# A PEER decoder layer on one core: map jobs begin earlier, weight splits a half unit later, a transfer on another queue, the last norm's splits placed by hand

## The chip, the cores and the metric

The kernel runs on one core of a Trainium2 chip. The metric is the time of one execution on the device in microseconds (us); less is better. Three runs of the kernel before took 2154.39 to 2157.17 us, median 2155.43 us. The profile comes from one more execution.

## What is computed

One decoder layer for T = 320 tokens (256 of a prompt, 64 of samples), D = 2048: a mixer (attention and a gated unit), then PEER, then a gated per-layer embedding (PLE). What matters here is PEER: each token picks 8 x 16 of 16384 experts, each expert being one row of `u_tab` and one of `v_tab`. The last two lines are the stage behind it.

```python
def one_block(xb):
    q = jnp.einsum('td,de->te', xb, wq).reshape(PEER_BLOCK, PEER_HEADS, 2, PEER_HALF)
    s1 = jnp.einsum('thc,nc->thn', q[:, :, 0], k1).astype(jnp.float32)
    s2 = jnp.einsum('thc,nc->thn', q[:, :, 1], k2).astype(jnp.float32)
    v1, i1 = lax.top_k(s1, PEER_TOPK)
    v2, i2 = lax.top_k(s2, PEER_TOPK)
    ...
    e = (jnp.take_along_axis(i1, ci // PEER_TOPK, axis=-1) * N_KEYS
         + jnp.take_along_axis(i2, ci % PEER_TOPK, axis=-1))
    g = jax.nn.softmax(sc, axis=-1).astype(xb.dtype)
    ue = jnp.take(u_tab, e, axis=0)
    act = jax.nn.gelu(jnp.einsum('thkd,td->thk', ue, xb))
    ve = jnp.take(v_tab, e, axis=0)
    return jnp.einsum('thk,thkd->td', g * act, ve)
...
h = h + peer(rmsnorm(h, norm_ffn), peer_wq, peer_k1, peer_k2, peer_u, peer_v)
gate = jax.nn.sigmoid(jnp.einsum('bld,de->ble', rmsnorm(h, ple_gate_norm), ple_gate_w))
h = h + jnp.einsum('blp,pd->bld', ple, ple_w) * gate
```

## The kernel before

**Units.** For 240 of the tokens the experts are computed densely. The tables are cut into 256 units of 1 MB: 128 u units (2048 x 128 of `u_tab`, then a gelu) and 128 v units. `order` lists them: 32 u units, then 16 groups of 8 v units with u units between. A unit has two halves, and a half two quarters. Float32 is made of two parts, so `prepare(n, h)` (L671) splits a half unit: a copy on ScalarE (ACT) gives `w_hi` (L683), a subtraction on VectorE (DVE) `w_lo` (L684). In its first half it also starts the unit's transfer `w_raw` on SyncE's queue. The pool of split halves has four buffers, so the split runs four half units ahead of `multiply(n, h, q)`, which issues a quarter: 12 matmuls on TensorE (PE), three for each of 4 chunks (`mm3`, L98 to L100). `finish(n)` (L702) evicts the unit's sum.

**The routing map.** Beside the first u units runs `front()`, the norm and the choice of the experts, a generator that tells its own cost in us at each `yield`; a loop gives it 1.4 us of such cost for each half unit. Then 30 jobs of 8 tokens build the map, the weight of each token for each expert. A job is `one_hots(j)`, two VectorE operations `e` (L762) and `p` (L763) in tiles with two buffers, and `map_products(j)`: 16 small matmuls (L775) in two groups, each with an eviction on ScalarE (L779). Every second job ends with a transfer `gd<-g_st` of 1 MB on GpSimd's (POOL) queue (L786). The one-hots of job j+1 are issued ahead of the products of job j. The jobs stand in ten half units (`first` to `U1` = 28), one or two behind each quarter, three in a half unit; `prepare(n + 2, h)` stands behind them.

**The routing weights.** Behind the map `fetch_g(0)` (L837) reads the first group's part of it back as `g_t` (960 KB, L839, on ScalarE's queue). `weights(g, gt)` (L842) is a generator of ten steps that multiplies the gelus with `g_t` (L854, VectorE) and splits the product in two (L865 ScalarE, L849 VectorE: `wh` and `wl`, or `a` and `c` for the first four). The v units multiply with these. `rows_of` (L791) makes rows of the other 80 tokens: copies `xd` on ScalarE (L801), transposes on TensorE (L798). For these tokens 160 steps (L819 a gather of rows on GpSimd's queue, L828 or L832 on VectorE) are spread over the units up to `END`, in proportion to the work planned.

**The last stage.** The pool of the PLE stage takes space that the last group's weights (`th`, `tl`) used. It loads `p_t` on GpSimd's queue (L1038), splits it in `p_h` (L118) and `p_l` (L121), multiplies with the embedding's weights (sums `ps_s`, evicted at L1046), splits the 16 chunks of the hidden state and sums their squares (L142, L143), and ends with 16 units of `w_gate`.

DVE, ACT and PE execute in the order of the code inside `manual_schedule`; the PLE stage stands behind it, and there a scheduler orders the work.

Of the kernel before, what the change touches and what calls it, by code (L numbers as in the profile page):

```python
# [10 lines left out]
F32 = mybir.dt.float32  # L11
# [41 lines left out]
def _build(ctx, tc, nc, a):  # L53
# [783 lines left out]
    def fetch_g(g):  # L837
        gt = vp.tile([P, NTB, GRP, 16], F32, name="g_t")
        nc.scalar.dma_start(gt.rearrange("p a b c -> p (a b c)"), gd[g])  # L839
        return gt  # L840

    def weights(g, gt):  # L842
# [4 lines left out]
        for i in range(GRP + 2):  # L847
# [9 lines left out]
            if 1 <= i <= GRP:  # L857
# [3 lines left out]
                elif k < 4:  # L861
                    w[k] = [flat4(up.tile([P, TD], F32R, tag="act", name=n, bufs=LEAD)) for n in ("th", "tl")]
# [5 lines left out]
    def add_samples():  # L868
        for c4 in range(2):
# [8 lines left out]
            )  # L878

# [11 lines left out]
    def front():  # L891
# [5 lines left out]
        yield 2.0  # L897
        shut(c_rt)
        state["xc"], xcp = open_pool("xc")
# [3 lines left out]
        yield 2.8  # L903
        one_hots(0)
        yield 2.8

    with tc.manual_schedule(engines={mybir.EngineType.DVE, mybir.EngineType.Activation, mybir.EngineType.PE}):
# [4 lines left out]
        steps = front()  # L912
        n, spent, slots = 0, 0.0, 0
        while steps:
            for h in range(2):
                multiply(n, h, 0)
                multiply(n, h, 1)
                if h == 0 and n:
                    finish(n - 1)
                slots += 1  # L920
                while steps and spent < 1.4 * slots:
                    cost = next(steps, None)
                    if cost is None:
                        steps = None
                    else:
                        spent += cost
                prepare(n + 2, h)
            n += 1

        first, job = n, 0  # L930
        while n < U1:
            for h in range(2):
                for q in range(2):
                    multiply(n, h, q)
                    if h == 0 and q == 0:
                        finish(n - 1)
                    at_ = (4 * (n - first) + 2 * h + q + 1) / (4 * (U1 - first))
                    while job < JOBS and job < round(JOBS * at_):
                        if job + 1 < JOBS:
                            one_hots(job + 1)  # L940
                        map_products(job)
                        job += 1
                prepare(n + 2, h)
            n += 1
# [20 lines left out]
        state["g"] = fetch_g(0)  # L965
# [3 lines left out]
        for n in range(n, LEAD):  # L969
            finish(n - 1)  # L970
            for h in range(2):
# [3 lines left out]
                if 2 * (n - U1) + h >= 5:  # L975
# [10 lines left out]
        END = len(order) - 7  # L986
# [5 lines left out]
        sums_x = None  # L992
        for n in range(LEAD, len(order)):
# [9 lines left out]
            for h in range(2):  # L1003
# [11 lines left out]
                if sums_x:  # L1015
                    next(sums_x, None)
                slots += 1
# [10 lines left out]
        finish(n)  # L1028
    shut(c_vp)
# [156 lines left out]
```

## Time and profile before

| | before |
|---|---|
| median of 3 runs | 2155.43 us (2154.39 to 2157.17) |
| profiled execution | 2153.34 us |
| its span | 2151.5 us |
| TensorE busy | 2103.3 us, 98% |
| VectorE busy | 1718.2 us, 80% |
| ScalarE busy | 1004.5 us, 47% |
| GpSimd busy | 323.8 us, 15% |

The span is the profiled execution without what lies around its first and last instruction. The granted clock is given as a share of TensorE's full speed (2.4 GHz); half of it is 1.2 GHz. A matmul's duration in the timeline overlaps the next one's; the distance of two starts is what it costs. In brackets stands how long the engine was idle before the instruction, and what ended the wait.

### The profile page before, as it was taken

Reading aid. Unit: us, or ns where it says so; the run is one execution under the profiler, and the core shown is the slowest. Engines: PE = TensorE matmul, PEld = TensorE weight load, DVE = VectorE, ACT = ScalarE, POOL = GpSimd, SP = SyncE. Lnnn points to the kernel's source line nnn. Section 1 sums busy time; section 2 is a strip of 40 time slices with the busy share of each in tenths; the row PEclk is TensorE's granted clock in tenths of the full one; section 3 lists DMA queues with packets and bytes.
Section 4 is the critical chain, followed back from the end, with each engine's and each line's share of the span. In section 5 each row is a group of like instructions: output and inputs, shape, how many; then the busy total and the mean of one; then the engine's idle time right before and its main releaser. Section 6 shows DMA issues by size and latency. Waiting matters only on the chain. (4 is left out here: it accounts for less than half of the span.)

```text
span 2151.5 us, 41052 instructions
## 1 busy us (share of the span) xinstructions
PE 2103.3 (98%) x17106; PEld 2053.0 (95%) x17106; DVE 1718.2 (80%) x2570; ACT 1004.5 (47%) x1465; POOL 323.8 (15%) x230
## 2 busy tenths in 40 slices
PE   8999999999998889999999999999999999999999
PEld 7878999999997879999999999999999999999998
DVE  6674875799997658888888888898898888886754
ACT  5346554335456655444444444444444444444632
POOL 2000000000001111221222222222222222120000
PEclk9999999999999889999999999999999999999999
DMA  7412354433555678998998989998898898895452
GB/s 279 144 59 99 115 182 172 140 121 137 188 203 168 201 255 311 365 345 333 387 353 340 376 349 336 360 374 350 336 377 338 349 383 355 312 367 181 161 181 83
DMA packets 85209, 563.06 MB, mean 262 GB/s; under 512 B 9894, under 2 KB 14438, under 8 KB 22160
## 3 DMA queue, kind: packets, MB, share of 16 engines
q1 hardware_dynamic: 49936, 349.76, 43.8%
q0 software_dynamic: 29536, 190.83, 23.4%
q10 hardware_dynamic: 5552, 19.86, 2.4%
q8 instruction: 134, 2.20, 0.4%
q14 instruction: 51, 0.42, 0.1%
HBM read 541.58 MB, written 19.79 MB: 261 GB/s over the span
## 5 line engine op out<-in xcount | busy, mean ns | idle before, releaser
L683 ACT ACTIVATE w_hi<-w_raw 128x1024 fp32r<-128x1024 f32 x512 | 542.8, 1061 | 698.9 <-PE ps_o L99 373.8
L684 DVE TENSOR_TENSOR w_lo<-w_raw,w_hi 128x1024 fp32r<-128x1024 f32 x512 | 625.3, 1222 | 218.9 <-ACT w_hi L683 216.1
L98 PE MATMUL ps_mm<-a,w_hi 128*128 128x240 f32 (+1 forms) x1776 | 519.6, 293 | 1.5 <-ACT w_hi L191 1.2
L99 PE MATMUL ps_mm<-a,w_hi 128*128 128x240 f32 (+1 forms) x1776 | 520.0, 293 | 1.0 <-DVE a L123 1.0
L100 PE MATMUL ps_mm<-a,w_lo 128*128 128x240 f32 (+1 forms) x1776 | 517.6, 291 | 2.6 <-DVE w_lo L684 2.1
L98 PE MATMUL ps_mm<-c,w_hi 128*128 128x240 f32 (+1 forms) x1280 | 361.6, 283 | 0.0
L100 PE MATMUL ps_mm<-c,w_lo 128*128 128x240 f32 (+1 forms) x1280 | 360.2, 281 | 0.0
L99 PE MATMUL ps_mm<-c,w_hi 128*128 128x240 f32 (+1 forms) x1280 | 359.9, 281 | 0.0
L99 PEld LDWEIGHTS ps_mm<-a,w_hi 128*128 128x128 f32 x1776 | 338.3, 190 | 8.9 <-issue 6.6
L98 PEld LDWEIGHTS ps_mm<-a,w_hi 128*128 128x128 f32 x1776 | 338.2, 190 | 7.8 <-issue 4.8
L100 PEld LDWEIGHTS ps_mm<-a,w_lo 128*128 128x128 f32 x1776 | 338.0, 190 | 7.0 <-issue 3.2
L81 ACT ACTIVATE w_hi<-w_raw 128x1024 fp32r<-128x1024 f32 x150 | 158.8, 1060 | 282.1 <-PE ps_mm L99 189.9
L99 PE MATMUL ps_o<-wl,w_hi 128*128 128x240 f32 x1024 | 282.9, 276 | 3.3 <-DVE wl L849 3.2
L100 PE MATMUL ps_o<-wh,w_lo 128*128 128x240 f32 x1024 | 283.0, 276 | 0.0
L98 PE MATMUL ps_o<-wh,w_hi 128*128 128x240 f32 x1024 | 279.7, 273 | 0.0
L82 DVE TENSOR_TENSOR w_lo<-w_raw,w_hi 128x1024 fp32r<-128x1024 f32 x150 | 183.0, 1223 | 89.5 <-ACT w_hi L81 86.3
L98 PEld LDWEIGHTS ps_mm<-c,w_hi 128*128 128x128 f32 x1280 | 242.8, 190 | 0.0
L100 PEld LDWEIGHTS ps_mm<-c,w_lo 128*128 128x128 f32 x1280 | 242.4, 189 | 0.2
L99 PEld LDWEIGHTS ps_mm<-c,w_hi 128*128 128x128 f32 x1280 | 242.5, 189 | 0.0
L99 PEld LDWEIGHTS ps_o<-wl,w_hi 128*128 128x128 f32 x1024 | 193.4, 189 | 4.2 <-DVE wl L849 4.0
L98 PEld LDWEIGHTS ps_o<-wh,w_hi 128*128 128x128 f32 x1024 | 194.8, 190 | 0.2 <-ACT wh L865 0.2
L100 PEld LDWEIGHTS ps_o<-wh,w_lo 128*128 128x128 f32 x1024 | 195.0, 190 | 0.0
(374 smaller groups left out, 3809.3 us busy)
## 6 DMA issues: line engine op xcount, KB each, us to landing
w_raw<-in_uT SPq DMA_DIRECT2D x128, 1024.0 KB
w_raw<-in_v_t SPq DMA_DIRECT2D x128, 1024.0 KB
w_raw<-in_w_in SPq DMA_DIRECT2D x25, 1024.0 KB
w_raw<-in_w_out SPq DMA_DIRECT2D x16, 1024.0 KB
w_raw<-in_wq SPq DMA_DIRECT2D x16, 1024.0 KB
w_raw<-in_w_gate SPq DMA_DIRECT2D x16, 1024.0 KB
gd<-g_st POOLq DMA_DIRECT2D x15, 1024.0 KB, 6.1
g_t<-gd ACTq DMA_DIRECT2D x16, 960.0 KB
```

The source lines that it names most:

```text
L81: last = act.activation(hi, s, AF.Copy)
L82: (lo_eng or vec).tensor_sub(lo, s, hi.bitcast(F32))
L98: pe.matmul(out, wh, xh, start=start, stop=False)
L99: pe.matmul(out, wh, xl, start=False, stop=False)
L100: pe.matmul(out, wl, xh, start=False, stop=stop)
L683: act.activation(hi, s, AF.Copy)
L684: vec.tensor_sub(lo, s, hi.bitcast(F32))
```

## The change

- The two loops for `front` and for the map become one over the 28 units. `front` tells less cost (1.4 for 2.0 and for 2.8; the last yield is gone), so that the jobs begin in half unit 42 instead of 46 and spread over 14 half units: two in each, but three in half units 45 and 52. In the map's half units `prepare` runs three half units ahead instead of four; half unit 41 prepares nothing, and one more `prepare` stands behind the loop.
- `fetch_g(0)` goes to GpSimd's queue. The other 15 stay on ScalarE's.
- `load`, the first group's `weights`, starts one half unit sooner.
- The last group's `th` and `tl` lie in one tile `thl` in the buffer of `xc`, which is done by then.
- `END` is ten units before the end of the order, not seven.
- `last_split()` puts the last norm's splits and squares by hand into the last seven v units, with squares of two chunks in one instruction; the loop in the PLE stage goes.

```diff
@@ -834,9 +834,9 @@
                 act.activation(self.w, self.a, AF.Gelu_apprx_tanh, scale=self.r)
                 vec.tensor_mul(self.w, self.w, self.g)
 
-    def fetch_g(g):
+    def fetch_g(g, queue=nc.scalar):
         gt = vp.tile([P, NTB, GRP, 16], F32, name="g_t")
-        nc.scalar.dma_start(gt.rearrange("p a b c -> p (a b c)"), gd[g])
+        queue.dma_start(gt.rearrange("p a b c -> p (a b c)"), gd[g])
         return gt
 
     def weights(g, gt):
@@ -859,7 +859,9 @@
                 if k < 4 and g < NG - 1:
                     w[k] = tails[k]
                 elif k < 4:
-                    w[k] = [flat4(up.tile([P, TD], F32R, tag="act", name=n, bufs=LEAD)) for n in ("th", "tl")]
+                    if k == 0:
+                        state["t"] = state["xcp"].tile([P, 8, TD], F32R, tag="xc", name="thl")
+                    w[k] = [flat4(state["t"][:, j]) for j in (2 * k, 2 * k + 1)]
                 else:
                     w[k] = [flat4(vp.tile([P, TD], F32R, name=n, bufs=GRP // 2)) for n in ("wh", "wl")]
                 act.activation(w[k][0], flat4(u[k]), AF.Copy)
@@ -877,6 +879,28 @@
                 pt.rearrange("p (c t) -> p c t", c=8),
             )
 
+    def last_split():
+
+        sq, total = {}, vp.tile([P, D], F32, tag="row", name="sqs", bufs=3)[:, : 2 * T].rearrange("p (a t) -> p a t", a=2)
+        for k in range(9):
+            if 2 <= k:
+                vec.tensor_add(total, total, sq.pop(k - 1))
+            if k < 8:
+                for c in (2 * k, 2 * k + 1):
+                    act.activation(xh(c)[0], hT[:, c], AF.Copy, scale=g_ple[:, c : c + 1])
+                yield
+                sq[k] = total
+                if k:
+                    t = vp.tile([P, D], F32, tag="row", name="sqs", bufs=3)
+                    sq[k] = t[:, : 2 * T].rearrange("p (a t) -> p a t", a=2)
+                act.activation(sq[k], hT[:, 2 * k : 2 * k + 2], AF.Square)
+                for c in (2 * k, 2 * k + 1):
+                    vec.scalar_tensor_tensor(
+                        xh(c)[1], hT[:, c], g_ple[:, c : c + 1], xh(c)[0].bitcast(F32), op0=ALU.mult, op1=ALU.subtract
+                    )
+                yield
+        vec.tensor_add(ssq, total[:, 0], total[:, 1])
+
     def add_first():
         pt = psum("tr", NC_ * XT)
         for c in range(NC_):
@@ -894,54 +918,52 @@
             yield from c
         yield from soften()
         picks = key_tables()
-        yield 2.0
+        yield 1.4
         shut(c_rt)
-        state["xc"], xcp = open_pool("xc")
+        state["xc"], state["xcp"] = open_pool("xc")
+        xcp = state["xcp"]
         state["rows"] = [xcp.tile([P, D], F32, name=n) for n in ("xc", "xx")]
         state["xd"] = lambda: xcp.tile([P, P], F32, name="xd", bufs=2)
         open_tables(picks)
-        yield 2.8
+        yield 1.4
         one_hots(0)
-        yield 2.8
 
     with tc.manual_schedule(engines={mybir.EngineType.DVE, mybir.EngineType.Activation, mybir.EngineType.PE}):
         for n in range(2):
             for h in range(2):
                 prepare(n, h)
 
-        steps = front()
-        n, spent, slots = 0, 0.0, 0
-        while steps:
+
+        steps, spent, job, first = front(), 0.0, 0, None
+        for n in range(U1):
             for h in range(2):
-                multiply(n, h, 0)
-                multiply(n, h, 1)
-                if h == 0 and n:
-                    finish(n - 1)
-                slots += 1
-                while steps and spent < 1.4 * slots:
-                    cost = next(steps, None)
-                    if cost is None:
-                        steps = None
-                    else:
-                        spent += cost
-                prepare(n + 2, h)
-            n += 1
-
-        first, job = n, 0
-        while n < U1:
-            for h in range(2):
+                slot = 2 * n + h
                 for q in range(2):
                     multiply(n, h, q)
-                    if h == 0 and q == 0:
+                    if h == 0 and q == 0 and n:
                         finish(n - 1)
-                    at_ = (4 * (n - first) + 2 * h + q + 1) / (4 * (U1 - first))
-                    while job < JOBS and job < round(JOBS * at_):
-                        if job + 1 < JOBS:
-                            one_hots(job + 1)
-                        map_products(job)
-                        job += 1
-                prepare(n + 2, h)
-            n += 1
+                    if first:
+                        at_ = (2 * (slot - first) + q + 1) / (2 * (2 * U1 - first))
+                        while job < JOBS and job < round(JOBS * at_):
+                            if job + 1 < JOBS:
+                                one_hots(job + 1)
+                            map_products(job)
+                            job += 1
+                if first:
+                    prepare((slot + 3) // 2, 1 - h)
+                else:
+                    while steps and spent < 1.4 * (slot + 1):
+                        cost = next(steps, None)
+                        if cost is None:
+                            steps = None
+                        else:
+                            spent += cost
+                    if steps:
+                        prepare(n + 2, h)
+                    else:
+                        first = slot + 1
+        prepare(U1 + 1, 1)
+        n = U1
         shut(oh["close"])
         c_vp, vp = open_pool("vp")
         c_xc, (xc, xx) = state["xc"], state["rows"]
@@ -962,7 +984,7 @@
                 rows[m] = k.fetch(j, second)
 
 
-        state["g"] = fetch_g(0)
+        state["g"] = fetch_g(0, pool)
         to_c = rows_of(xc, state["xd"], slice(TP, T), 2)
         to_x = rows_of(xx, state["xd"], slice(0, XT), PH)
         load = weights(0, state["g"])
@@ -972,7 +994,7 @@
                 for q in range(2):
                     multiply(n, h, q)
                     next(to_c, None)
-                if 2 * (n - U1) + h >= 5:
+                if 2 * (n - U1) + h >= 4:
                     for _ in range(3):
                         next(load, None)
                 if n == LEAD - 1 and h == 0:
@@ -983,13 +1005,14 @@
             pass
 
 
-        END = len(order) - 7
+        END = len(order) - 10
         extra = lambda n: 0.65 * (order[n - 1][0] == "v")
         step_us = 2.4
         total = sum(extra(n) for n in range(LEAD, END)) + 0.8 * GRP * NG + step_us * len(steps)
         m, spent, slots = 0, 0.0, 0
         sums_c = add_samples()
         sums_x = None
+        last_norm = last_split()
         for n in range(LEAD, len(order)):
             finish(n - 1)
             if order[n][0] == "v" and order[n][2] == 0:
@@ -1014,6 +1037,8 @@
                     next(sums_c, None)
                 if sums_x:
                     next(sums_x, None)
+                if order[n][0] == "v" and order[n][1] == NG - 1 and order[n][2]:
+                    next(last_norm)
                 slots += 1
                 while m < len(steps) and (spent + step_us / 2 < total * slots / (2 * (END - LEAD)) or n >= END):
                     k, j, second = steps[m]
@@ -1026,6 +1051,8 @@
                 if n + 2 < len(order):
                     prepare(n + 2, h)
         finish(n)
+        for _ in last_norm:
+            pass
     shut(c_vp)
     shut(c_xc)
     shut(c_up)
@@ -1044,9 +1071,6 @@
             for c in range(2):
                 mm3(pp, w_ple(2 * (o % 8) + c), p_hl[0][:, c], p_hl[1][:, c], c == 0, c == 1)
             act.activation(emb[:, o], pp, AF.Copy)
-        for c in range(NC_):
-            hilo(xh(c), hT[:, c], g_ple[:, c : c + 1])
-            square_sum(pl, ssq, hT[:, c], c == 0)
         pm = psum("tr", T)
         pe.matmul(pm, ones_d, ssq, start=True, stop=True)
         r = rstd(pl, pm, T)
```

VectorE's queue at the start of the map. L743 and L750 belong to `front`; `w_lo` is a split, `e` and `p` the one-hots of one job. Before:

```order
L743 CAST i_6912<-c_iota 128x512
L750 SCALAR_TENSOR_TENSOR sel_6914<-ps_tr,sel_6914 128x16x8
L750 SCALAR_TENSOR_TENSOR sel_6915<-ps_tr,sel_6915 128x16x8
L684 TENSOR_TENSOR w_lo<-w_raw,w_hi 128x1024 x2
L762 TENSOR_TENSOR e<-i_6912,sel_6914 128x2048
L763 TENSOR_TENSOR p<-e,sel_6914 128x2048
L684 TENSOR_TENSOR w_lo<-w_raw,w_hi 128x1024 x4
L762 TENSOR_TENSOR e<-i_6912,sel_6914 128x2048
L763 TENSOR_TENSOR p<-e,sel_6914 128x2048
L762 TENSOR_TENSOR e<-i_6912,sel_6914 128x2048
L763 TENSOR_TENSOR p<-e,sel_6914 128x2048
L762 TENSOR_TENSOR e<-i_6912,sel_6914 128x2048
```

And after:

```order
L743 CAST i_6912<-c_iota 128x512
L750 SCALAR_TENSOR_TENSOR sel_6914<-ps_tr,sel_6914 128x16x8
L750 SCALAR_TENSOR_TENSOR sel_6915<-ps_tr,sel_6915 128x16x8
L684 TENSOR_TENSOR w_lo<-w_raw,w_hi 128x1024
L762 TENSOR_TENSOR e<-i_6912,sel_6914 128x2048
L763 TENSOR_TENSOR p<-e,sel_6914 128x2048
L762 TENSOR_TENSOR e<-i_6912,sel_6914 128x2048
L763 TENSOR_TENSOR p<-e,sel_6914 128x2048
L762 TENSOR_TENSOR e<-i_6912,sel_6914 128x2048
L763 TENSOR_TENSOR p<-e,sel_6914 128x2048
L684 TENSOR_TENSOR w_lo<-w_raw,w_hi 128x1024
L762 TENSOR_TENSOR e<-i_6912,sel_6914 128x2048
```

One split less stands ahead of the first one-hots, which are followed at once by those of jobs 1 and 2; between two splits stand two jobs' one-hots from there on, where three jobs' stood.

ScalarE's queue at the end of the map. `g_st` are evictions of map products, `act` a gelu, `xd` a copy for a transpose. Before:

```order
L683 ACTIVATE w_hi<-w_raw 128x1024
L779 ACTIVATE g_st<-ps_o 128x4x128 x2
L779 ACTIVATE g_st<-ps_s 128x4x128 x2
L779 ACTIVATE g_st<-ps_o 128x4x128 x2
L683 ACTIVATE w_hi<-w_raw 128x1024
L839 DMA g_t<-gd 128x1920
L706 ACTIVATE act<-ps_mm 128x240
L801 ACTIVATE xd<-hT,c_gains 128x128 x2
L683 ACTIVATE w_hi<-w_raw 128x1024
L801 ACTIVATE xd<-hT,c_gains 128x128 x2
```

And after:

```order
L779 ACTIVATE g_st<-ps_s 128x4x128 x2
L779 ACTIVATE g_st<-ps_o 128x4x128 x2
L683 ACTIVATE w_hi<-w_raw 128x1024
L779 ACTIVATE g_st<-ps_s 128x4x128 x2
L779 ACTIVATE g_st<-ps_o 128x4x128 x2
L683 ACTIVATE w_hi<-w_raw 128x1024 x2
L706 ACTIVATE act<-ps_mm 128x240
L801 ACTIVATE xd<-hT,c_gains 128x128 x2
L683 ACTIVATE w_hi<-w_raw 128x1024
L801 ACTIVATE xd<-hT,c_gains 128x128 x2
```

The transfer `g_t` is gone from between the last split and the gelu, two splits stand together, and two jobs lie between splits. On GpSimd's queue it stands behind the map's transfers and ahead of the row gathers, after:

```order
L737 DMA x_eg<-ex 16x2x16 x8
L786 DMA gd<-g_st 128x16x128 x15
L839 DMA g_t<-gd 128x1920
L819 DMA row<-in_u_rows,c_e 128x2048 x64
L819 DMA row<-in_u_rows,x_eg 128x2048 x16
L819 DMA row<-in_v_rows,c_e 128x2048 x64
L819 DMA row<-in_v_rows,x_eg 128x2048 x16
L1065 DMA p_t<-in_pT 128x640
```

In before L839 is not in this queue and the gathers follow the map's transfers; the rest stands as here.

ScalarE's queue ahead of the last stage. L81 is a split of the embedding's or the gate's weights, L118 and L890 the high parts of the hidden state's chunks `c` and of `p_t`, L142 and L896 squares. Before:

```order
L81 ACTIVATE w_hi<-w_raw 128x1024 x2
L118 ACTIVATE c<-hT,c_gains 128x320 x2
L81 ACTIVATE w_hi<-w_raw 128x1024
L142 ACTIVATE sq<-hT 128x320 x6
L118 ACTIVATE p_h<-p_t 128x640
L142 ACTIVATE sq<-hT 128x320 x2
L81 ACTIVATE w_hi<-w_raw 128x1024
L142 ACTIVATE sq<-hT 128x320
L1046 ACTIVATE emb<-ps_s 128x320
```

And after:

```order
L81 ACTIVATE w_hi<-w_raw 128x1024 x2
L890 ACTIVATE c<-hT,c_gains 128x320 x2
L896 ACTIVATE sqs<-hT 128x640
L81 ACTIVATE w_hi<-w_raw 128x1024
L118 ACTIVATE p_h<-p_t 128x640
L81 ACTIVATE w_hi<-w_raw 128x1024
L890 ACTIVATE c<-hT,c_gains 128x320 x2
L896 ACTIVATE sqs<-hT 128x640
L1073 ACTIVATE emb<-ps_s 128x320 x3
```

The six squares ahead of `p_h` have become one of twice the width and the copies of two chunks, with two splits of weights behind them; evictions `emb` stand behind two more copies and a square.

## Rows read from the trace of the kernel before

**Rows 1.** the page's first line: busy time, share of the span, instructions

```profile
PE 2103.3 (98%) x17106; PEld 2053.0 (95%) x17106; DVE 1718.2 (80%) x2570; ACT 1004.5 (47%) x1465; POOL 323.8 (15%) x230
```

**Rows 2.** windows: us; busy us of PE, PEld, DVE, ACT, POOL; clock; DMA; GB/s

```profile
650.00:764.00 114.00, 95.34 (x741) 90.32 (x739) 81.64 (x69) 70.16 (x76) 17.37 (x15) 0.87 0.59 178
764.00:771.00 7.00, 0.15 (x2) 0.15 (x2) 0.33 (x1) 0.86 (x4) 1.72 (x2) 0.72 0.94 291
796.00:801.00 5.00, 2.85 (x14) 2.80 (x14) 4.40 (x5) 2.95 (x6) 0.38 (x1) 0.67 0.86 320
801.00:820.00 19.00, 19.00 (x156) 19.00 (x156) 12.91 (x14) 8.59 (x13) 4.66 (x3) 0.91 0.66 241
820.00:1960.00 1140.00, 1139.72 (x10191) 1139.53 (x10189) 992.77 (x1012) 513.55 (x647) 269.51 (x154) 1.00 0.91 351
```

**Rows 3.** timeline of PE in the map

```profile
650.75 2.05 PE L775 MATMUL ps_s<-p,e 128*128 128x128 f16 x16
666.04 2.05 PE L775 MATMUL ps_s<-p,e 128*128 128x128 f16 x16 [1.11 <-DVE p L763]
677.96 0.36 PE L98 MATMUL ps_mm<-a,w_hi 128*128 128x240 f32 x1
680.39 2.09 PE L775 MATMUL ps_s<-p,e 128*128 128x128 f16 x16
682.23 0.36 PE L98 MATMUL ps_mm<-c,w_hi 128*128 128x240 f32 x1
688.13 2.06 PE L775 MATMUL ps_s<-p,e 128*128 128x128 f16 x16 [1.08 <-DVE p L763]
759.06 2.06 PE L775 MATMUL ps_o<-p,e 128*128 128x128 f16 x16 [0.34 <-DVE p L763]
```

**Rows 4.** timeline of ACT in the map

```profile
683.36 1.06 ACT L683 ACTIVATE w_hi<-w_raw 128x1024 fp32r<-128x1024 f32 x1
```

**Rows 5.** timeline of DVE at the map's start and in it

```profile
637.19 1.22 DVE L684 TENSOR_TENSOR w_lo<-w_raw,w_hi 128x1024 fp32r<-128x1024 f32 x1 [0.17 <-ACT w_hi L683]
684.46 1.23 DVE L684 TENSOR_TENSOR w_lo<-w_raw,w_hi 128x1024 fp32r<-128x1024 f32 x1 [3.58 <-ACT w_hi L683]
```

**Rows 6.** timeline of POOL, ACT and PE at the first read of the map

```profile
762.62 1.15 POOL L786 DMA_DIRECT2D gd<-g_st  x1 [5.69 <-ACT g_st L779]
769.76 0.33 ACTq L839 DMA_DIRECT2D g_t<-gd  x1
770.14 0.37 ACT L706 ACTIVATE act<-ps_mm 128x240 f32<-128x240 f32 x1 [7.06 <-DMA gd<-g_st]
770.85 0.47 PE L798 MATMUL ps_tr<-ident,xd 128*128 128x128 f32 x1 [7.05 <-ACT xd L801]
```

**Rows 7.** the map's transfers by tile: durations ns, first and last start, landing

```profile
L786 POOL DMA_DIRECT2D gd<-g_st x15: 1152/1152/1212, 657.7 to 762.6; - x15
DMA to landing us min/median/max: 6.0/6.1/6.8
```

**Rows 8.** timeline of DVE and PE, first group's weights to their first use

```profile
786.25 0.72 DVE L854 TENSOR_TENSOR act<-act,g_t 128x240 f32<-128x240 f32 x2
797.75 0.40 DVE L849 TENSOR_TENSOR wl<-act,wh 128x240 fp32r<-128x240 f32 x1
798.20 0.57 PE L99 MATMUL ps_o<-wl,w_hi 128*128 128x240 f32 x1 [2.15 <-DVE wl L849]
```

**Rows 9.** timeline of ACT and PE before the last stage

```profile
2010.11 1.06 ACT L81 ACTIVATE w_hi<-w_raw 128x1024 fp32r<-128x1024 f32 x1 [0.31 <-ACT c L118]
2015.50 0.74 ACT L118 ACTIVATE p_h<-p_t 128x640 fp32r<-128x640 f32 x1 [0.38 <-DMA p_t<-in_pT]
2016.29 0.64 PE L98 MATMUL ps_s<-p_h,w_hi 128*128 128x320 f32 x1 [3.46 <-ACT p_h L118]
```

**Rows 10.** waits from 2004 to 2022 us: in total, times, longest

```profile
POOL p_t L1038 <- PE ps_o L100: 81.0, 1, 81.0
```

## The prediction, made before the changed kernel had run

> **What bounds the kernel now.** The page's first line comes first: TensorE is busy 98% of the span [rows 1], so only what makes it stand, or run at a lower clock, can move the time; VectorE (80%) and ScalarE (47%) count only where TensorE waits for them. The table of windows then says where it stands [rows 2]. From 820 to 1960 us it is busy 1139.72 of 1140 us at full clock: nothing is to be had there, only lost. The losses lie in four places that the change touches. While the routing map is built (650 to 764) TensorE is busy 95.34 of 114 us at a granted clock of 0.87. From 764 to 771 it does nothing. From 796 to 801 it is busy 2.85 us of 5 at clock 0.67, and 801 to 820 still shows 0.91. The fourth is a wait before the last stage [rows 9].
>
> The map first, from TensorE's timeline [rows 3]. A job (16 small matmuls) starts at 680.39 and the weight matmuls behind it at 682.23, so it holds TensorE for 1.84 us. A quarter is 12 weight matmuls; the one from 677.96 to 680.39 took 2.43 us, mostly at half clock. At full clock a matmul takes 1139.72 / 10191 = 0.112 us [rows 2], a quarter 1.34. Two quarters and two jobs are thus 6.4 us of TensorE. But the job at 688.13 starts 7.74 us after the one at 680.39, and waits 1.08 us for the one-hot product `p`. The chain between them [rows 4, 5]: job at 680.39; its evictions on ScalarE; behind them in ScalarE's queue the high half `w_hi` at 683.36 (+2.97); the low half `w_lo` on VectorE at 684.46 (+4.07); behind it the next job's `e` and `p`; the job at 688.13 (+7.74). So the split of the weights stands in the middle of the map's own chain, once in each half unit.
>
> **The map's schedule.** There are 30 jobs. Before, ten half units carry three each; after, fourteen half units, the first one four half units sooner, carry two each, but for two that carry three. The split is half a unit later, so half unit 41 splits nothing, and one `w_lo` that stood ahead of the first one-hots goes. Splitting later does not shorten the chain: in the order `w_hi` still stands behind the evictions, `w_lo` behind `w_hi`, and the one-hots behind `w_lo`. What the change does is to put each such chain beside two jobs instead of three, and to begin sooner.
> - First job. `w_lo` of 637.19 takes 1.22 us and ends at 638.4; from the end of that of 684.46 (685.7) to the job at 688.13, one-hots take 2.45 [rows 5]. So job 0 can start at 640.9 instead of 650.75 [rows 3]. Its half unit begins four half units of 2.68 us before 649.41 (650.75 less 1.34), at 638.7, and its quarter ends at 640.0: it waits 0.9 us.
> - Job 1, after one more quarter and one-hots that are ready: 640.9 + 1.84 + 1.34 = 644.1.
> - Then eleven half units of two jobs at 7.74 us = 85.1, and two of three jobs. Six jobs, two half units of before, take 666.04 to 688.13 = 22.1 us. So job 29 starts at 644.1 + 85.1 + 22.1 = 751.3 instead of 759.06: **-7.8 us**.
> TensorE has 1.3 us of slack in each half unit (7.74 - 6.4), so one quarter as slow as that of 677.96 (+1.1) is covered.
>
> **The first routing weights.** After the last job ScalarE's queue holds the issue of `g_t`, which waits for the last map transfer to land: ScalarE stands 7.06 us, and the transposes for TensorE stand behind it, so TensorE stands 7.05 us until 770.85 [rows 6]. Issued from GpSimd's queue it waits there instead; queued behind it are only the row gathers, whose rows VectorE first takes after 798. What is late next is ScalarE itself: from job 29's start its evictions (+2.97 by the chain above), two `w_hi` (1.06 each), a gelu and `xd` put the first transpose at about +5.6, against +1.84 and two quarters (+4.5) of TensorE: 1.1 to 1.3 us of the wait stay, **-5.7 us**. The clock of 0.72 there cost 3 us at half speed after 770.85; I take **-0.5 us**, since a gap stays.
>
> Does `g_t` land in time? Before, the last map transfer is issued at 762.62 (3.56 us after job 29) and has landed by 769.76 (10.7 after it). So GpSimd begins the issue at 751.3 + 10.7 = 762.0; an issue takes 1.15 us and landing 6.0 to 6.8 us for 1024 KB [rows 7]: 769.2 to 769.9. The first product with `g_t` starts at 786.25 in before [rows 8], 27.2 us after job 29; less the stall (5.7), a half unit (2.9, next part) and 0.5 that is +18.1, or 769.4. The products then have some 2 us more before TensorE needs their last result.
>
> One rule of the Trainium skill speaks against this move. The rows first: fifteen transfers of 1024 KB went out from GpSimd's queue among VectorE's one-hots, at 1152 to 1212 ns an issue and 6.0 to 6.8 us to land [rows 7], so VectorE held them up by 0.8 us at most. By "SBUF — State Buffer", section "Who interferes with whom", a transfer from GpSimd's queue can starve while VectorE works in a two-port mode, and one from ScalarE's queue can't, though the page excepts two-input operations such as the ones here. By the rule `g_t` would be late by as much as VectorE holds the port; by the row it isn't, and I go by the row.
>
> **The weights one half unit sooner.** Before, `wl` of 797.75 comes 2.15 us late for the matmul at 798.20 [rows 8], and the clock then falls: 0.67 in 796 to 801 (5 x 0.33 = 1.6, of which 0.2 lies in the wait) and 0.91 in 801 to 820 (19 x 0.09 = 1.7), 3.1 us lost [rows 2]. Starting a half unit (2.9 us) sooner, and with 12 instead of 9 turns so that nothing is left over, covers 2.15: **-2.15 and -3.1 us**.
>
> **The last norm.** Before, TensorE stands 3.46 us until 2016.29, since `p_h` at 2015.50 stands behind squares and behind the transfer of `p_t`, which waits for the last matmul of the v units [rows 9, 10]. After, `p_t` waits for ScalarE alone. A square of 640 columns (0.74 us, as `p_h`'s copy) stands ahead of the `w_hi` of 2010.11 and `p_h` right behind it: 2010.11 + 0.74 + 1.06 = 2011.9, or 2012.5 if the square waits; the first matmul comes at about 2013.0, but `p_l`, one more step on VectorE, and the evictions, behind one more chunk's copies, hold the next groups. Bounds: 0, if all that is given back, and -5, the whole wait and 1.5 us for the low clock that may follow a wait, as after 770.85; the nearest row is the wait of 3.46, less 1.5 for what is late next: **-2 us**.
>
> **The long stretch.** END three units earlier packs 160 steps 1.4% closer (3 of 217 units). VectorE is busy 992.77 of 1140 us there [rows 2]; covered by its 147 idle us, I take 0. Without the cover see the last rival. The new tiles for the last group and squares add no instruction that TensorE waits for: 0.
>
> **Sum.** -7.8 - 5.7 - 0.5 - 2.15 - 3.1 - 2 = -21.3 us. The profiled execution took 2153.34 us (span 2151.5) and would take 2132.1; the runs' median is 2155.43, 2.1 higher, so 2134.
>
> **Rivals.**
> - TensorE becomes the bound of the map: 6.4 instead of 7.74 us in a half unit, 13 x 1.3 = 17 less, some 2118. For it: jobs are sparser. Against it: the order leaves the chain whole.
> - `g_t` comes late on GpSimd's queue: the gap and low clock at `wl` stay (+5.25), 2139.5, and each us beyond another, to about 2143. For it: no margin but 2 us, and the stretch 764 to 771 has its transfers 94% busy [rows 2]. Against: 6.0 to 6.8 us in fifteen cases.
> - The waits of 1.1 to 1.3 us in each half unit bring the clock down through the whole map: two quarters at half clock (2 x 2.69) and two jobs are 9.06 us, 1.32 over 7.74: 13 x 1.32 = 17, some 2151, hardly faster. For it: before has slow quarters, as that of 677.96. Against: over the whole map of before, which has waits of 1.08 and 1.11 too, the clock is 0.87 [rows 2, 3].
> - Slower than before: the denser steps push VectorE behind, and at each of 15 groups `wl` is late as at 797.75. That wait with its clock cost 5.3 us; from 21.3 / 15 = 1.4 us a group the gain is gone, and at half the price, 2.7, the time is 2134 + 40 = 2174. Against it: TensorE idles 0.28 us in 1140 now.
>
> **Chances.** Forecast 0.62, TensorE bound 0.07, `g_t` late 0.16, low clock throughout 0.09, denser steps 0.06. A change under 0.2%, 4.3 us, can't be told from none. The forecast's own range is 2127 to 2140 (the last norm 0 to -5, the map's clock and first job +-4). For 8 in 10 I take in most of the late `g_t` and half of the faster rival: 2121 to 2145. Faster: 0.62 + 0.07 + 0.16 + half of 0.09 = 0.90; same 0.05; slower 0.05.
>
> **What would show it.** Right: jobs 7.7 us apart over a half unit, the first near 641 and the last near 751; ScalarE never waiting for the map's transfer, TensorE's gap there 1 to 1.5 us; no wait for `wl` at the first v unit; the wait for `p_h` under 1 us. Wrong: a product waiting for `g_t`, half clock in every half unit of the map, or waits for `wl` or `w_lo` between 820 and 1960.

## The result, and the profile after

The changed kernel takes 2135.67 us, the median of 4 runs (2133.95 to 2139.41), against 2155.2 us before (4 runs, 2154.39 to 2157.17): a ratio of 0.991, 95% interval 0.9893 to 0.9928. That is 19.5 us less; 2134 were forecast. Its profiled execution took 2136.97 us.

The page's first line for the changed kernel, against [rows 1]: TensorE's busy time is 2.1 us less, the span 16.3 us less. So most of what went is TensorE's standing still.

```profile
span 2135.2 us, 41032 instructions
...
PE 2101.2 (98%) x17106; PEld 2051.5 (96%) x17106; DVE 1714.6 (80%) x2563; ACT 1002.7 (47%) x1457; POOL 315.1 (15%) x231
```

The table of windows (columns as in [rows 2]), first of a stretch far ahead of the change, then of the map, what follows it, and the last stage:

```profile
184.00:194.00 10.00, 9.94 (x44) 8.11 (x44) 1.29 (x4) 4.34 (x26) 0.00 (x0) 0.66 0.00 2
643.00:755.00 112.00, 99.12 (x798) 95.08 (x798) 84.45 (x72) 71.00 (x77) 16.22 (x14) 0.94 0.62 187
755.00:761.00 6.00, 6.00 (x41) 5.99 (x39) 2.36 (x2) 5.45 (x8) 1.15 (x1) 0.72 0.83 280
761.00:781.00 20.00, 19.83 (x176) 19.45 (x174) 12.22 (x21) 14.95 (x33) 3.51 (x4) 1.00 0.99 385
781.00:786.00 5.00, 4.18 (x36) 4.03 (x37) 4.49 (x4) 3.98 (x8) 0.00 (x0) 1.00 1.01 424
806.00:1944.00 1138.00, 1137.72 (x10173) 1137.54 (x10173) 989.83 (x1012) 513.19 (x647) 260.94 (x155) 1.00 0.91 351
1996.00:2008.00 12.00, 9.21 (x42) 8.21 (x40) 9.47 (x13) 7.92 (x14) 0.00 (x0) 0.72 0.51 176
```

The same for before, of the first and the last of these stretches:

```profile
184.00:194.00 10.00, 9.88 (x63) 8.10 (x61) 2.02 (x6) 6.26 (x41) 0.00 (x0) 1.00 0.00 0
2012.00:2024.00 12.00, 8.32 (x47) 7.61 (x45) 10.01 (x19) 10.03 (x22) 0.38 (x1) 0.86 0.48 182
```

In the map TensorE is busy 99.12 of 112 us; the 7 us in which it did nothing are gone (6.00 of 6.00, at a low clock); at the first v unit 4.18 of 5 us and no low clock. The first row matters for reading all the rest: this execution ran at clock 0.66 from 184 to 194 us, where before's ran at 1.00, and lost 2.3 us before it came to anything that the change touches. So executions are compared here by stretches. Both kernels run the same 15936 weight matmuls (L98 to L100), in the same order but for some of the last stage; a stretch is the time from one of them to another, less the same in before. The borders are, in before and after: 603.56 and 605.83; the first one behind the last job, 760.87 and 755.71; the first v unit's first, 793.00 and 782.20; 809.85 and 793.29; 1944.70 and 1928.12; and the last, 2145.99 and 2130.03. The map, for one: (755.71 - 605.83) - (760.87 - 603.56) = -7.4 us. Without the 2.3 us ahead of the change the execution of after is 18.2 us shorter than that of before, for the 21.3 of the forecast.

| us against before | ahead | map | map's end to first v unit | first v unit | long stretch | last stage | sum |
|---|---|---|---|---|---|---|---|
| forecast | 0 | -7.8 | -6.2 | -5.25 | 0 | -2 | -21.3 |
| after | +2.3 | -7.4 | -5.6 | -5.8 | 0.0 | +0.6 | -16.0 |
| e1, map alone | -0.2 | -7.3 | +0.8 | -1.4 | +0.8 | +0.3 | -7.0 |
| e2, `g_t` on ScalarE | +3.3 | -7.4 | +2.3 | -5.8 | 0.0 | +0.7 | -6.9 |
| e3, weights later | +0.8 | -7.4 | -7.0 | -1.4 | +1.0 | +0.2 | -13.9 |
| e4, old last norm | -0.2 | -5.7 | -3.7 | -5.8 | 0.0 | +0.3 | -15.1 |
| e5, split early | +0.8 | -7.4 | -3.3 | -5.8 | +0.9 | +0.6 | -14.1 |
| e6, split between | +0.3 | -22.2 | -3.4 | -5.8 | 0.0 | +0.1 | -30.9 |
| e7, split ahead | -0.5 | -5.2 | -3.5 | -5.8 | +0.9 | -0.2 | -14.1 |
| e8, norm behind | +0.6 | -5.8 | -3.7 | -5.8 | +1.5 | -1.5 | -14.6 |
| e9, three edits | +0.5 | -24.2 | -6.3 | -5.8 | +1.6 | -2.4 | -36.5 |
| e10, two edits | -0.2 | -22.5 | -3.7 | -5.8 | 0.0 | -2.4 | -34.5 |
| e11, four turns | +0.5 | -7.4 | -6.1 | -5.8 | +1.3 | -0.8 | -18.3 |

In the column of the map, e4, e8 and e10 carry 1.6 us that no edit made: half clock came before their first job (0.83 from 620 to 630 us, 1.00 in after), and that job starts 38.9 us behind the first border instead of 37.3.

TensorE's timeline in the map of after, against [rows 3]: the first job, some in the middle, the last.

```profile
643.13 2.03 PE L775 MATMUL ps_s<-p,e 128*128 128x128 f16 x16 [0.67 <-DVE p L763]
646.34 2.06 PE L775 MATMUL ps_o<-p,e 128*128 128x128 f16 x16
...
654.07 2.06 PE L775 MATMUL ps_o<-p,e 128*128 128x128 f16 x16 [1.07 <-DVE p L763]
657.31 2.06 PE L775 MATMUL ps_s<-p,e 128*128 128x128 f16 x16
661.80 2.07 PE L775 MATMUL ps_o<-p,e 128*128 128x128 f16 x16 [1.08 <-DVE p L763]
...
753.90 2.06 PE L775 MATMUL ps_o<-p,e 128*128 128x128 f16 x16 [1.09 <-DVE p L763]
```

Less the 2.3 us of the start, job 0 is at 640.9, job 1 at 644.1 and the last at 751.6; forecast were 640.9, 644.1 and 751.3. From 654.07 to 661.80 it is 7.73 us, with one wait for `p` in each half unit.

### The profile page after: what moved, and what is told of

The parts are those of the page before. It is cut to its first block, busy times and chain, and to the rows that moved or that the text cites. A ratio compares the mean times of both kernels' runs of the same rounds, so it can differ in the third digit from the quotient of the medians.

```text
span 2135.2 us, 41032 instructions
## 1 busy us (share of the span) xinstructions
PE 2101.2 (98%) x17106; PEld 2051.5 (96%) x17106; DVE 1714.6 (80%) x2563; ACT 1002.7 (47%) x1457; POOL 315.1 (15%) x231
## 5 line engine op out<-in xcount | busy, mean ns | idle before, releaser
L98 PE MATMUL ps_mm<-a,w_hi 128*128 128x240 f32 (+1 forms) x1776 | 518.2, 292 | 2.1 <-ACT w_hi L191 1.7
L100 PE MATMUL ps_mm<-a,w_lo 128*128 128x240 f32 (+1 forms) x1776 | 516.6, 291 | 2.6 <-DVE w_lo L684 2.1
L98 PE MATMUL ps_mm<-c,w_hi 128*128 128x240 f32 (+1 forms) x1280 | 362.9, 283 | 0.0
L100 PE MATMUL ps_mm<-c,w_lo 128*128 128x240 f32 (+1 forms) x1280 | 361.2, 282 | 0.0
L98 PEld LDWEIGHTS ps_mm<-a,w_hi 128*128 128x128 f32 x1776 | 336.8, 190 | 8.4 <-issue 4.8
L100 PEld LDWEIGHTS ps_mm<-a,w_lo 128*128 128x128 f32 x1776 | 336.8, 190 | 7.0 <-issue 3.2
L81 ACT ACTIVATE w_hi<-w_raw 128x1024 fp32r<-128x1024 f32 x150 | 158.6, 1059 | 282.2 <-PE ps_mm L99 188.8
L100 PE MATMUL ps_o<-wh,w_lo 128*128 128x240 f32 x1024 | 282.3, 276 | 0.0
L98 PE MATMUL ps_o<-wh,w_hi 128*128 128x240 f32 x1024 | 278.9, 272 | 0.0
L100 PEld LDWEIGHTS ps_mm<-c,w_lo 128*128 128x128 f32 x1280 | 243.4, 190 | 0.2
L98 PEld LDWEIGHTS ps_mm<-c,w_hi 128*128 128x128 f32 x1280 | 243.5, 190 | 0.0
L98 PEld LDWEIGHTS ps_o<-wh,w_hi 128*128 128x128 f32 x1024 | 194.3, 190 | 0.0
L100 PEld LDWEIGHTS ps_o<-wh,w_lo 128*128 128x128 f32 x1024 | 194.3, 190 | 0.0
```

The source lines that it names most:

```text
L81: last = act.activation(hi, s, AF.Copy)
L98: pe.matmul(out, wh, xh, start=start, stop=False)
L100: pe.matmul(out, wl, xh, start=False, stop=stop)
```

## The experiments

**e1, the map alone.** Before, with the merged loop and the yields of the change and nothing else of it:

```diff
-        yield 2.8
         one_hots(0)
-        yield 2.8
...
+                if first:
+                    prepare((slot + 3) // 2, 1 - h)
```

> The kernel before with the map's new schedule alone. If each part acts by itself: two jobs 7.7 us apart per half unit, the last job 7 to 8 us earlier than in before, and behind it TensorE's wait of 7 us for g_t and the late wl of about 2 us with its low clock as in before; about 2147.5 us. If the earlier jobs only pay together with the transfer's queue: the wait behind the map grows by what the map saves; 2154 to 2156 us.

It took 2146.38 us beside a run of before of 2157.65. The map gave 7.3 us, and TensorE's timeline shows the old waits behind it, as in [rows 6, 8]:

```profile
763.02 0.48 PE L798 MATMUL ps_tr<-ident,xd 128*128 128x128 f32 x1 [6.71 <-ACT xd L801]
...
791.46 0.38 PE L99 MATMUL ps_o<-wl,w_hi 128*128 128x240 f32 x1 [2.15 <-DVE wl L849]
```

The parts act by themselves. (The late `wl` cost less than in before: the half clock behind it was shorter, and the first v unit took 15.48 us at a mean clock of 0.89, against 16.85 at 0.80.)

**e2, the transfer's queue.**

```diff
-        state["g"] = fetch_g(0, pool)
+        state["g"] = fetch_g(0)
```

> The changed kernel with the first g_t back on ScalarE's queue. If ScalarE's wait for the map's last transfer is the cost: ScalarE stands about 7 us again, TensorE with it, and the changed kernel's time grows by 6 to 7 us, to 2142; more, up to 5, if wl is late too. If the queue is indifferent, because the data is waited for either way: under 1 us, 2136.

It took 2146.43 us, above the 2142 expected, and 3.3 us of it came ahead of the change (first column). The stretch behind the map is 7.9 us longer than in after. ScalarE's timeline has the wait again:

```profile
757.91 2.00 ACT L683 ACTIVATE w_hi<-w_raw 128x1024 fp32r<-128x1024 f32 x2
765.33 0.33 ACTq L839 DMA_DIRECT2D g_t<-gd  x1
765.71 0.37 ACT L706 ACTIVATE act<-ps_mm 128x240 f32<-128x240 f32 x1 [5.80 <-DMA gd<-g_st]
```

So the queue is worth 7.9 us there against after's execution, and 5.6 to 6.0 against e4, e5, e7 and e8, in which `g_t` came late from GpSimd's queue (see e4); `wl` was not late.

**e3, the weights one half unit later.**

```diff
-                if 2 * (n - U1) + h >= 4:
+                if 2 * (n - U1) + h >= 5:
```

> The changed kernel with the first group's weights begun one half unit later, as before. If the half unit is what removed the wait: wl comes 1.5 to 3 us late at the first v unit and half clock follows; about 5 us more, 2141. If the earlier map alone made room (g_t no longer holds ScalarE): wait under 0.5 us, 2136.

It took 2138.99 us. `wl` is 2.15 us late, to the hundredth what it was before:

```profile
784.52 0.38 PE L99 MATMUL ps_o<-wl,w_hi 128*128 128x240 f32 x1 [2.15 <-DVE wl L849]
```

That costs 4.4 us at the first v unit; but the stretch ahead of it is 1.4 us shorter than in after, so the earlier start is worth 3.0 us net there, not 5.25. Against e4, e5, e7 and e8, where `g_t` came late, it is worth 0.6 to 1.1 us. What it gives back is seen in e4.

**e4, the old last norm.** The changed kernel without `last_split` and `thl`, with

```diff
-        END = len(order) - 10
+        END = len(order) - 7
```

> The changed kernel with the last norm, th and tl, and END as before. If the hand-placed splits gave back by a cycle of 5.9 us per v unit what they took out of the wait: TensorE's wait for p_h is 3.3 to 3.6 us again, no v unit takes more than 5.4 us between two additions to hT, and the end comes within 0.8 us of the changed kernel's; 2135. If they gained the 2 us of the prediction: 2137.5 to 2138.

It took 2137.87 us. The last stage costs +0.3 with the old norm, here and in e1. With the new one it costs +0.6 in after and -0.8 to +0.7 in the six other runs that leave it as it is (e2, e3, e5, e6, e7, e11): no gain stands out, and none of 2 us. The lowest of them, e11, is the one without half clock there (1.00 from 1995 to 2007 us). TensorE's wait for `p_h` is back at 3.41 us, and most additions to `hT` are again 5.39 us apart. It also showed this, on VectorE and then TensorE:

```profile
772.31 0.73 DVE L854 TENSOR_TENSOR act<-act,g_t 128x240 f32<-128x240 f32 x2 [2.41 <-DMA g_t<-gd]
```

```profile
774.77 0.33 PE L798 MATMUL ps_tr<-ident,xd 128*128 128x128 f32 x1 [1.30 <-ACT xd L801]
778.94 0.33 PE L798 MATMUL ps_tr<-ident,xd 128*128 128x128 f32 x1 [1.05 <-ACT xd L801]
782.99 0.62 PE L798 MATMUL ps_tr<-ident,xd 128*128 128x128 f32 x2 [0.92 <-ACT xd L801]
```

`g_t`, issued at 764.13, landed 8.2 us later, and the first product waited 2.41 us for it; ScalarE waited for the product, and TensorE for the copies `xd` behind it. The same happened in e5, e7 and e8, and with other orders of the map in e6 and e10. In the profiled execution of after `g_t`, issued at 764.78, landed 4.8 us later, and the product found it there:

```profile
771.15 0.72 DVE L854 TENSOR_TENSOR act<-act,g_t 128x240 f32<-128x240 f32 x2
```

Of TensorE's three waits only the last is there too (0.92 us), and also in e2, where no product waited: it belongs to the earlier start of the weights, not to a late `g_t`. What brought `g_t` in time in after isn't shown. It is not the low clock behind the map by itself: in the 8 us behind the last job the clock was 0.79 in after and in e5, and e5's product waited 2.32 us. The transfer `w_raw` of a unit, issued 0.7 us behind `g_t` in after, took 9.7 us to land; issued together with `g_t` in e4, it took 5.0.

**e5, the split as early as before.** In the new schedule, four half units ahead:

```diff
-                    prepare((slot + 3) // 2, 1 - h)
+                    prepare(n + 2, h)
...
-                    if steps:
-                        prepare(n + 2, h)
-                    else:
+                    prepare(n + 2, h)
+                    if not steps:
                         first = slot + 1
-        prepare(U1 + 1, 1)
```

> The changed kernel with the split four half units ahead, as before, in the new map schedule. If the later split is no part of the gain (the chain eviction, w_hi, w_lo, one-hots is the same): jobs again 7.74 us apart per half unit, job 0 later by 1.1 us or less, the last job later by 0 to 1.5 us; 2135 to 2138 us. If the later split is what makes room: half units of the map longer than 7.74 us, 5 us or more in sum; 2140 or more.

It took 2138.83 us; the map gives 7.4 us as in after, and job 0 is as early. That the split comes a half unit later is no part of the gain.

**e6, the split between one-hots and products.** In each half unit of the map:

```diff
+                        early = q == 0
...
                             if job + 1 < JOBS:
                                 one_hots(job + 1)
+                            if early:
+                                prepare((slot + 3) // 2, 1 - h)
+                                early = False
                             map_products(job)
                             job += 1
-                if first:
-                    prepare((slot + 3) // 2, 1 - h)
-                else:
+                if not first:
```

> The changed kernel with the half unit's split moved, in the map, between the one-hots and the products of the half unit's first job: w_hi then stands behind the evictions of the job before and w_lo ahead of one-hots that are wanted three jobs after it. If the chain job, eviction, w_hi, w_lo, one-hots, job of 7.74 us bounds the map: it then covers one and a half half units, TensorE's own 6.4 to 6.5 us become the bound, and the last job comes 11 to 15 us sooner than in the changed kernel; about 2123 us. If something else bounds it (evictions, the map's transfers with their two buffers, a low clock): under 5 us.

It took 2121.94 us. In TensorE's timeline no job waits for `p` but the first (0.67 us), and most half units take 6.48 us (654.09 to 660.57); two waits for evictions stay, of 1.81 and 1.55 us:

```profile
654.09 2.05 PE L775 MATMUL ps_s<-p,e 128*128 128x128 f16 x16
657.33 2.06 PE L775 MATMUL ps_o<-p,e 128*128 128x128 f16 x16
660.57 2.07 PE L775 MATMUL ps_s<-p,e 128*128 128x128 f16 x16
...
716.92 2.06 PE L775 MATMUL ps_o<-p,e 128*128 128x128 f16 x16 [1.55 <-ACT g_st L779]
...
737.14 2.06 PE L775 MATMUL ps_o<-p,e 128*128 128x128 f16 x16
```

The map is 14.8 us shorter than in after. With it `g_t` is late by 3.75 us.

**e7, the split ahead of the one-hots too.** As e6, but with the three lines from `if early` on ahead of `if job + 1 < JOBS`.

> As the one before, but the split stands ahead of the first job's one-hots too. By the same chain: w_lo stands ahead of one-hots that are wanted one half unit after the job whose evictions it waits for, so half units of 7.7 us stay; the last job within 2 us of the changed kernel's; 2134 to 2138 us. If any split ahead of the first job's evictions is enough: 11 to 15 us sooner; 2123.

It took 2138.76 us, and the waits are back:

```profile
651.62 2.05 PE L775 MATMUL ps_o<-p,e 128*128 128x128 f16 x16 [1.09 <-DVE p L763]
654.86 2.06 PE L775 MATMUL ps_s<-p,e 128*128 128x128 f16 x16
659.63 2.06 PE L775 MATMUL ps_o<-p,e 128*128 128x128 f16 x16 [1.38 <-DVE p L763]
```

Between e6 and e7 one VectorE instruction stands two places elsewhere, and 17 us lie between their maps. Since both move the split ahead of the first job's evictions, it is the chain through the one-hots that bounds the map, as [rows 3 to 5] were read.

**e8, the last norm behind the split.**

```diff
-                if order[n][0] == "v" and order[n][1] == NG - 1 and order[n][2]:
-                    next(last_norm)
...
                 if n + 2 < len(order):
                     prepare(n + 2, h)
+                if order[n][0] == "v" and order[n][1] == NG - 1 and order[n][2]:
+                    next(last_norm)
```

> The changed kernel with each step of the last norm behind the half unit's split instead of ahead of it. If the cycle of 5.88 us (addition to hT, two copies c, w_hi, w_lo, the low parts of c, w_lo, next addition) against TensorE's 5.36 made VectorE late: additions to hT 5.3 to 5.4 us apart, p_h 2 to 3 us sooner against the last v matmul, TensorE's wait for it under 1 us; 2 to 5.5 us gained. If something else holds p_h (the last addition, the splits' buffers): within 0.7 us of the changed kernel.

It took 2138.31 us, for a late `g_t` and 1.5 us in the long stretch; the last stage alone is 2.1 us shorter than in after. Additions to `hT` in the middle units are 5.37 to 5.44 us apart, and the wait for `p_h` is 0.80 us. Of `p_h` itself 2 to 3 us were expected; it comes 1.2 us sooner, 0.3 us behind the last v matmul instead of 1.5. The rest of the 2.1 goes in part with a shorter half clock: where neither execution had half clock in this place, in e10 and e11 (below), the edit's gain is 1.5 us. VectorE and TensorE:

```profile
1975.92 0.65 DVE L710 TENSOR_TENSOR hT<-hT,ps_o 128x480 f32<-128x480 f32 x1
1981.31 0.65 DVE L710 TENSOR_TENSOR hT<-hT,ps_o 128x480 f32<-128x480 f32 x1
1986.68 0.65 DVE L710 TENSOR_TENSOR hT<-hT,ps_o 128x480 f32<-128x480 f32 x1
```

```profile
2000.48 0.41 PE L98 MATMUL ps_s<-p_h,w_hi 128*128 128x320 f32 x1 [0.80 <-ACT p_h L118]
```

**e9, e10 and e11.** e10 is e6 with e8; e9 has this edit too, and e11 is the changed kernel with it alone:

```diff
-                if 2 * (n - U1) + h >= 4:
-                    for _ in range(3):
+                if 2 * (n - U1) + h >= 5:
+                    for _ in range(4):
```

> The changed kernel with three edits: the split between one-hots and products (as e6), the last norm behind the split (as e8), and the first group's weights begun one half unit later but in four turns each. If the three terms add: 14 to 15 us from the map, 1.5 to 2.5 from the last norm, 2 to 5 from no longer waiting for g_t; 2115 to 2119 us, ratio to before 0.982. If weights in four turns come late at the first v unit: 2120 to 2123.

> The changed kernel with the split between one-hots and products and the last norm behind the split, without the edit of the weights. If these two add and g_t is still late: 2119 to 2121 us, and TensorE waits 2 to 3 us for a transpose behind g_t. If the map's gain is given back later: 2125 or more.

> The changed kernel with the first group's weights begun one half unit later, but in four turns instead of three. If g_t lands too late for the earlier start in most runs and the fourth turn makes up for the later one: no product waits for g_t, no wait for wl at the first v unit, and from the map's end to the first v unit 2 to 3 us less than in the runs where g_t was late; 2133 to 2136 us. If four turns crowd VectorE: wl late again by 1 us or more, 2138 or above.

e9 took 2116.89 us, median of 5 runs (2116.28 to 2118.63), a ratio to before of 0.9824 (0.981 to 0.9837); e10 2118.57 us, 0.9838 (0.9822 to 0.9855); e11 2134.6 us in one run. The terms add. In e11 and e9 the stretch ahead of the first v unit is 2.4 to 2.6 us shorter than in e4 or e10, and `wl` is in time. e9 has the lowest median here, 0.9% under the changed kernel's; its lead on e10 is within the noise (2116.28 to 2118.63 us against 2117.82 to 2124.4). Its wait for `g_t` on VectorE is down to this:

```profile
754.77 0.73 DVE L854 TENSOR_TENSOR act<-act,g_t 128x240 f32<-128x240 f32 x2 [0.73 <-DMA g_t<-gd]
```

## Why the prediction was right, and where not

Of the 3.1 us by which after's execution falls short of the forecast (18.2 for 21.3), the last norm makes 2.6.

**The map's schedule: right**, in size and in mechanism: -7.4 for -7.8, jobs within 0.3 us of where they were put, and the chain of 7.74 us confirmed by e6 and e7. e5 confirms that the later split adds nothing. The rival in which TensorE becomes the bound had its price about right (17 us, against 14.8 in e6), and needed another order, as was said. The low clock through the whole map didn't come: 0.94 against 0.87 before.

**The first routing weights: right**, -5.6 for -6.2. ScalarE no longer waits. ScalarE's and GpSimd's timelines behind the map:

```profile
756.85 2.00 ACT L683 ACTIVATE w_hi<-w_raw 128x1024 fp32r<-128x1024 f32 x2
758.75 0.36 ACT L706 ACTIVATE act<-ps_mm 128x240 f32<-128x240 f32 x1
759.00 0.69 ACT L801 ACTIVATE xd<-hT,c_gains 128x128 f32<-128x128 f32 x2
```

```profile
757.47 1.15 POOL L786 DMA_DIRECT2D gd<-g_st  x1 [6.57 <-ACT g_st L779]
764.78 0.56 POOL L839 DMA_DIRECT2D g_t<-gd  x1 [6.16 <-PE ps_tr L798]
765.65 1.04 POOL L819 DMA_INDIRECT row<-in_u_rows,c_e  x1 [0.30 <-issue]
```

The copies `xd` begin at 759.00, and the first transpose stands at 760.11, 6.2 us behind the last job, for the 5.6 of the forecast; TensorE, at the low clock, came to it no sooner and did not wait. At full clock, in e4, e8 and e11, it waited 0.8 us there, for the 1.1 to 1.3 of the forecast. That the whole stretch agrees so well is luck in part: it rests on a `g_t` that landed early in this one execution (next paragraph), and is -3.3 to -3.7 in e4, e5, e7 and e8.

**Whether `g_t` lands in time: right that the margin is next to nothing, but by luck.** The sum (landing at 769.2 to 769.9, wanted at 769.4) added the issue's 1.15 us to landing times that count from the issue's start already: in e4, 764.13 and 8.2 us make 772.3, and the product starts at 772.31. Without that, `g_t` would have been 0.6 to 1.4 us early. The runs moved both ends: landing took 8.1 to 8.5 us in e4 to e11, not 6.0 to 6.8, and apart from `g_t` the first product could have started 15.8 to 17.3 us behind the last job, not 18.1, in the runs with the change's start of the weights.

And the lateness was held to be free for some 2 us, since the products have that much time before TensorE needs the last of them. It is not free. ScalarE's copies `xd` stand behind those of the weights, so TensorE waits for a transpose as soon as a product waits for `g_t`. That is the rival with 0.16, by another path and at 2 to 3 us instead of 5: the six runs with `g_t` over 2 us late are 1.9 to 2.4 us worse in this stretch than after.

The transfer took 8.2 us in e4 where the map's took 6.0 to 6.8 [rows 7]; while it runs, from 764 to 772 us, the transfers' share is 0.98, against 0.59 in the map of before [rows 2]. But in after it is 0.95 from 764 to 770 us, where 4.8 us sufficed. That the other transfers, the row gathers behind it among them, make it slower was not tried alone. The Trainium skill's rule ("SBUF — State Buffer", section "Who interferes with whom") doesn't show: the issue took 0.56 us, less than the map's transfers, and from ScalarE's queue, in e1 and e2, `g_t` took longer to land (9.2 and 9.3 us).

**The weights one half unit sooner: right in mechanism**, -5.8 for -5.25 at the first v unit; but 1.4 us of it is the longer half clock of before's execution, which e1 and e3 had not, with the same wait of 2.15 us. Net of what the earlier start gives back it is worth less; e3 and e11 show it.

**The last norm: wrong.** The step that failed is "-2", with its place for `p_h` at 2011.9 to 2012.5. Measured from the last v matmul, that is 0.1 to 0.7 us ahead of it (2012.56 in before); `p_h` came 1.5 us behind it (1997.71 against 1996.21; before 2.9). So it came 1.4 us sooner than before, not 3.0 to 3.6; the wait of 2.00 us that was left, one of 0.79 for `p_l` and a lower clock (0.72 from 1996 to 2008, against 0.86 from 2012 to 2024 in before) ate the gain: +0.6. The working took ScalarE's copies to be ready when they had been before. But the splits by hand tie ScalarE and VectorE in a circle. VectorE in after, one turn of it:

```profile
1966.55 0.65 DVE L710 TENSOR_TENSOR hT<-hT,ps_o 128x480 f32<-128x480 f32 x1
1969.23 1.22 DVE L684 TENSOR_TENSOR w_lo<-w_raw,w_hi 128x1024 fp32r<-128x1024 f32 x1 [2.03 <-ACT w_hi L683]
1970.37 1.01 DVE L898 SCALAR_TENSOR_TENSOR a<-hT,c_gains,a 128x320 fp32r<-128x320 f32 x2
1971.30 1.22 DVE L684 TENSOR_TENSOR w_lo<-w_raw,w_hi 128x1024 fp32r<-128x1024 f32 x1
1972.43 0.65 DVE L710 TENSOR_TENSOR hT<-hT,ps_o 128x480 f32<-128x480 f32 x1
```

And ScalarE in it, with the end of the chain:

```profile
1967.23 1.02 ACT L890 ACTIVATE a<-hT,c_gains 128x320 fp32r<-128x320 f32 x2 [2.35 <-DVE hT L710]
1968.15 1.04 ACT L683 ACTIVATE w_hi<-w_raw 128x1024 fp32r<-128x1024 f32 x1
...
1997.71 0.72 ACT L118 ACTIVATE p_h<-p_t 128x640 fp32r<-128x640 f32 x1
```

The addition to `hT` (1966.55) lets ScalarE copy two chunks (1967.23), behind them stands `w_hi` (1968.15), behind it on VectorE `w_lo`, the chunks' low parts, another `w_lo`, and then the next addition (1972.43): 5.88 us, where TensorE's unit, 48 weight matmuls, takes 5.38 (1969.10 to 1974.48). The additions fall 0.5 us further behind with each unit. TensorE shows no wait there that before hasn't, and part of the sum is paid at the stage's border. e8 breaks the circle by putting each step behind the split: `p_h` comes 1.2 us sooner, and the stage is 1.5 to 2.1 us shorter.

**The long stretch: right**, 0.0. In seven experiments a wait or two of 0.4 to 1.3 us for an addition to `hT` made 0.8 to 1.6 us there, also in e1, which has the old END, and none in after's execution, e2, e4, e6 and e10. So the closer steps are not needed for it; what makes it isn't shown.

## What to carry to other kernels

Where an operation of one engine stands in a queue between two of another's, look for the circle that it closes, and divide its length by the work that passes in one turn: moving one instruction by two places made a turn cover three jobs instead of two. A circle that is only some tenths longer than the bound engine's period may show no wait of that engine for a while, as here until the border of the stage; check its period against that engine's, not its waits. A transfer whose landing has no margin costs at the first engine that has other work queued behind its consumer.

## What the runs showed of the hardware that was not expected

- Half clock came and went between executions in places where nothing was changed: 0.66 from 184 to 194 us in after, 1.00 in before, for 2.3 us; 0.83 from 620 to 630 us in e4, e8 and e10, 1.00 in after, for 1.6 us. That is as much as the last norm was to bring, so terms of 2 us were read from stretches.
- With a wait for `p` of mostly 1.07 to 1.13 us in nearly every half unit, the mean clock in the map of after was 0.94; in e9, nearly without waits, it was 0.98.
- The first `g_t`, 960 KB, took 4.8 to 8.5 us to land from GpSimd's queue and 9.2 and 9.3 us from ScalarE's (e1, e2), with the transfers 95% busy or more in after and e4; the map's transfers of 1024 KB in before took 6.0 to 6.8 us, with 59%.
